# A small load on 120 partitions moved from the front of the load queue to second place, and its square from ScalarE to VectorE

The chip is one Trainium2, of which one core is used. The metric is the time of one execution in device microseconds.

## The reference

The input `x` is fp32, 32 x 256 x 4096. Of every four neighbouring values the root of the mean square is taken (p = 2), so the output is 32 x 256 x 1024:

```python
for i in range(out_length):
    window = np.abs(x[:, :, 4*i:4*i + 4]) ** p
    result[:, :, i] = (np.mean(window, axis=-1)) ** (1.0 / p)
```

134.22 MB are read and 33.55 MB are written. There is very little arithmetic for each byte.

## The kernel before

The input is treated as one flat row of values. Nearly all of it is loaded in 22 large loads, most of them 128 partitions x 13184 values (6.75 MB), into three slots. ScalarE squares a load in three chunks, VectorE sums groups of four, ScalarE takes the root, and the results of two loads are stored at once. The 22 loads leave 840 x 128 values over, the "piece". It is 430 KB, 0.3% of the input. It lies on 120 partitions of 896 values and has its own load, sums and store.

```python
def load(i):
    ...
    nc.sync.dma_start(out=v, in_=block(xf, g, 1)[:, src:src + w])
...
def root(g, o, ends):
    nc.scalar.activation(out=o, in_=o, func=Act.Sqrt, scale=1.0 / k)
    if ends and g not in late:
        store(g, nc.scalar)
...
Q = 120
odd = ODD * P // Q
t = o_tiles[1][0:Q, 0:odd]
nc.sync.dma_start(out=t, in_=xf[(total - ODD) * P:total * P].rearrange("(p w) -> p w", p=Q))
ahead = 0
while ahead < n and loads[ahead][0] < X_SLOTS:
    load(ahead)
    ahead += 1
nc.scalar.activation(out=t, in_=t, func=Act.Square)
o = o_tiles[1][0:Q, odd:odd + odd // k]
nc.vector.tensor_reduce(
    out=o, in_=t.rearrange("p (n j) -> p n j", j=k),
    axis=mybir.AxisListType.X, op=mybir.AluOpType.add,
)
nc.scalar.activation(out=o, in_=o, func=Act.Sqrt, scale=1.0 / k)
nc.scalar.dma_start(
    out=of[(total - ODD) * P // k:total * P // k].rearrange("(p w) -> p w", p=Q), in_=o,
)
...
for i in range(n):
    ...
    for step in chunks:
        v = xs[i][:, c:c + step]
        nc.scalar.activation(out=v, in_=v, func=Act.Square)
        total_sum(ots[g][:, summed:summed + step // k], v, i)
        while pending and pending[0][0] <= done - LAG:
            root(*pending.pop(0)[1:])
        ...
```

## Time and profile before

| | before |
|---|---|
| time, median of 3 runs | 394.59 us (394.59 to 394.62) |
| span of the profiled run | 392.8 us |
| VectorE busy | 271.8 us (69%) |
| ScalarE busy | 292.5 us (74%) |
| bytes moved, mean rate | 167.79 MB, 427 GB/s |

### The profile page before, as it was taken

What the parts mean: (1) busy time and instruction counts of PE and PEld (TensorE: products, weight loads), DVE (VectorE), ACT (ScalarE), POOL (GpSimd) and SP (SyncE); (2) the same over time, 40 slices, a digit from 0 to 9 for tenths busy, and PEclk for the clock granted to TensorE, in tenths of its full rate; (3) what the DMA queues carried; (4) which work ended last, traced back from release to release, by engine and by line L of the source; (5) the groups of instructions that cost most, each with busy time, mean ns of one, the idle gap of its engine ahead of it and who ended that gap; (6) DMA issues with size and microseconds to landing.
All of it is one profiled execution on the core that took longest, in us unless ns stands there. A gap on an engine that the chain in (4) does not pass through costs nothing.

```text
span 392.8 us, 341 instructions
## 1 busy us (share of the span) xinstructions
DVE 271.8 (69%) x77; ACT 292.5 (74%) x128; POOL 0.2 (0%) x4
## 2 busy tenths in 40 slices
DVE  1059989594959495949594959495949494778781
ACT  3088987776776777677867786868586859899990
POOL 0000000000000000000000000000000000000000
DMA  9999999999999989999999999999999999999997
GB/s 361 420 429 446 446 446 384 430 470 430 389 432 473 430 387 435 467 430 422 432 435 430 427 435 427 430 435 459 459 404 430 459 438 430 395 430 432 429 432 315
DMA packets 5024, 167.79 MB, mean 427 GB/s; under 512 B 558, under 2 KB 678, under 8 KB 926
## 3 DMA queue, kind: packets, MB, share of 16 engines
q1 hardware_dynamic: 3879, 144.04, 85.2%
q10 hardware_dynamic: 1143, 23.73, 14.0%
q14 instruction: 2, 0.02, 0.0%
HBM read 134.22 MB, written 33.55 MB: 427 GB/s over the span
## 4 chain that ended last, share of the span: by engine, by line
DMA 62%; ACT 21%; DVE 10%; issue 4%; SPq 0%; ACTq 0%
DMA xt<-in_x_dram 62%; ACT xt L143 17%; DVE ot L96 8%; ACT ot L89 3%; ACT xt L89 1%; DVE xt L105 1%; DVE xt L106 0%; ACTq L86 0%; SPq L80 0%; SPq L112 0%; ACTq L89 0%
## 5 line engine op out<-in xcount | busy, mean ns | idle before, releaser
L143 ACT ACTIVATE xt<-xt 128x4384 f32<-128x4384 f32 (+4 forms) x62 | 229.6, 3705 | 85.1 <-DMA xt<-in_x_dram 81.9
L96 DVE TENSOR_REDUCE ot<-xt 128x1096 f32<-128x4384 f32 (+1 forms) x48 | 227.0, 4731 | 90.1 <-ACT xt L143 89.8
L89 ACT ACTIVATE ot<-ot 128x1096 f32<-128x1096 f32 (+1 forms) x54 | 59.8, 1107 | 1.8 <-DVE ot L96 1.1
L105 DVE TENSOR_TENSOR xt<-xt 128x1648 f32<-128x1648 f32 (+4 forms) x14 | 28.4, 2032 | 16.0 <-ACT xt L143 16.0
L89 ACT ACTIVATE xt<-xt 128x824 f32<-128x824 f32 (+2 forms) x8 | 6.5, 817 | 1.9 <-DVE xt L106 1.9
L106 DVE TENSOR_TENSOR ot<-xt 128x1096 f32<-128x1096 f32 (+1 forms) x6 | 7.8, 1303 | 0.2
L106 DVE TENSOR_TENSOR xt<-xt 128x824 f32<-128x824 f32 (+2 forms) x8 | 7.5, 939 | 0.3
L119 DVE TENSOR_REDUCE ot<-ot 120x224 f32<-120x896 f32 x1 | 1.1, 1086 | 5.7 <-ACT ot L117 5.7
L117 ACT ACTIVATE ot<-ot 120x896 f32<-120x896 f32 x1 | 0.9, 949 | 2.7 <-DMA ot<-in_x_dram 2.7
L117 ACT ACT_TABLE_LOAD x1 | 1.3, 1283 | 0.7 <-PEq L174 0.7
L123 ACT ACT_TABLE_LOAD x1 | 1.3, 1283 | 0.0
L123 ACT ACTIVATE ot<-ot 120x224 f32<-120x224 f32 x1 | 0.4, 389 | 0.0
L174 POOL MEMSET const-bfloat16-1.0<- 128x1 bf16 x1 | 0.1, 101 | 0.0
L174 POOL MEMSET const-uint8-127<- 128x1 uint8 x1 | 0.1, 101 | 0.0
L174 POOL MEMSET const-float32-0.0<- 128x1 f32 x1 | 0.1, 99 | 0.2 <-issue 0.2
L174 POOL MEMSET const-float32-1.0<- 128x1 f32 x1 | 0.1, 99 | 0.0
## 6 DMA issues: line engine op xcount, KB each, us to landing
xt<-in_x_dram SPq DMA_DIRECT2D x18, 6592.0 KB, 39.9
out_dram<-ot ACTq DMA_DIRECT2D x7, 3296.0 KB, 27.6
xt<-in_x_dram SPq DMA_DIRECT2D x3, 3296.0 KB, 29.4
out_dram<-ot SPq DMA_DIRECT2D x2, 3296.0 KB, 30.0
out_dram<-xt SPq DMA_DIRECT2D x1, 2472.0 KB, 10.4
xt<-in_x_dram SPq DMA_DIRECT2D x1, 2108.0 KB, 26.8
out_dram<-xt SPq DMA_DIRECT2D x1, 527.0 KB, 7.1
ot<-in_x_dram SPq DMA_DIRECT2D x1, 420.0 KB, 4.0
```

The source lines that it names most:

```text
L89: nc.scalar.activation(out=o, in_=o, func=Act.Sqrt, scale=1.0 / k)
L96: nc.vector.tensor_reduce(out=o, in_=v.rearrange("p (n j) -> p n j", j=k), axis=mybir.AxisListType.X, op=add,)
L105: nc.vector.tensor_tensor(out=h, in0=q[:, :, 0:2], in1=q[:, :, 2:4], op=add)
L106: nc.vector.tensor_tensor(out=o, in0=h[:, :, 0], in1=h[:, :, 1], op=add)
L117: nc.scalar.activation(out=t, in_=t, func=Act.Square)
L119: nc.vector.tensor_reduce(out=o, in_=t.rearrange("p (n j) -> p n j", j=k), axis=mybir.AxisListType.X, op=mybir.AluOpType.add,)
L123: nc.scalar.activation(out=o, in_=o, func=Act.Sqrt, scale=1.0 / k)
L143: nc.scalar.activation(out=v, in_=v, func=Act.Square)
L174: nc = _bacc.Bacc("TRN2", target_bir_lowering=False, num_devices=1)
```

## The change

The piece is loaded second, behind the first large load, so that the large load starts sooner. Its square goes to VectorE, and its compute is placed behind the first Square of the first large load. The bytes, the sums and the store stay.

```diff
-    t = o_tiles[1][0:Q, 0:odd]
-    nc.sync.dma_start(out=t, in_=xf[(total - ODD) * P:total * P].rearrange("(p w) -> p w", p=Q))
-    ahead = 0
+    odd_x = o_tiles[1][0:Q, 0:odd]
+    odd_o = o_tiles[1][0:Q, odd:odd + odd // k]
+    load(0)
+    nc.sync.dma_start(
+        out=odd_x, in_=xf[(total - ODD) * P:total * P].rearrange("(p w) -> p w", p=Q),
+    )
+    ahead = 1
...
-    nc.scalar.activation(out=t, in_=t, func=Act.Square)
...
+    def odd_sum():
+        nc.vector.tensor_tensor(out=odd_x, in0=odd_x, in1=odd_x, op=mybir.AluOpType.mult)
+        nc.vector.tensor_reduce(
...
+    def odd_root():
+        nc.scalar.activation(out=odd_o, in_=odd_o, func=Act.Sqrt, scale=1.0 / k)
+        nc.scalar.dma_start(
...
             nc.scalar.activation(out=v, in_=v, func=Act.Square)
+            if i == 0 and c == 0:
+                odd_sum()
             total_sum(ots[g][:, summed:summed + step // k], v, i)
             while pending and pending[0][0] <= done - LAG:
                 root(*pending.pop(0)[1:])
+            if i == 0 and c == 0:
+                odd_root()
```

More of the change, by code (lines that the diff above doesn't have):

```diff
@@ L116 @@
         ahead += 1
-    nc.scalar.activation(out=t, in_=t, func=Act.Square)
-    o = o_tiles[1][0:Q, odd:odd + odd // k]
-    nc.vector.tensor_reduce(
-        out=o, in_=t.rearrange("p (n j) -> p n j", j=k),
-        axis=mybir.AxisListType.X, op=mybir.AluOpType.add,
-    )
-    nc.scalar.activation(out=o, in_=o, func=Act.Sqrt, scale=1.0 / k)
-    nc.scalar.dma_start(
-        out=of[(total - ODD) * P // k:total * P // k].rearrange("(p w) -> p w", p=Q), in_=o,
-    )
+    def odd_sum():
+        nc.vector.tensor_tensor(out=odd_x, in0=odd_x, in1=odd_x, op=mybir.AluOpType.mult)
+        nc.vector.tensor_reduce(
+            out=odd_o, in_=odd_x.rearrange("p (n j) -> p n j", j=k),
+            axis=mybir.AxisListType.X, op=mybir.AluOpType.add,
+        )
+    def odd_root():
+        nc.scalar.activation(out=odd_o, in_=odd_o, func=Act.Sqrt, scale=1.0 / k)
+        nc.scalar.dma_start(
+            out=of[(total - ODD) * P // k:total * P // k].rearrange("(p w) -> p w", p=Q),
+            in_=odd_o,
+        )
     pending = []
```

## The prediction

> **What bounds the kernel now.** I first read the page's row of DMA share and the line on HBM traffic, then a table of stretches (busy time of each engine, DMA share, GB/s), then the chain of work that ended last, then the waits.
>
> ```profile
> DMA  9999999999999989999999999999999999999997
> HBM read 134.22 MB, written 33.55 MB: 427 GB/s over the span
> 20.00:340.00 320.00, 236.03 (x53) 246.34 (x101) 0.00 (x0) 1.00 1.00 431
> 340.00:380.00 40.00, 31.55 (x21) 38.96 (x20) 0.00 (x0) 1.00 1.01 432
> ```
>
> In the last two lines the columns are the stretch, its length, busy us of VectorE, ScalarE and GpSimd, the clock, the DMA share and GB/s. The transfers are full from 20 to 380 us, while VectorE is busy 74% (236/320) and ScalarE 77% (246/320). All 167.77 MB of input and output have to pass; at 431 GB/s that alone is 389 us of the 392.8 us span. What is left is the start (until data flows) and the end (the last results). The chain agrees: 62% of it is loads in flight. Its one long stretch of compute is the end: from 340.62 to 384.79 ScalarE runs almost without a gap, on loads that have landed, while late stores keep the transfers busy. That stretch starts when the load of 340.6 lands, so a delay or gain in the stream of loads should pass to the end, and one that only shifts compute in an early stage should not.
>
> The change touches only the first 45 us, so I looked at the timeline there.
>
> ```profile
> 0.72 1.28 ACT L117 ACT_TABLE_LOAD   x1 [0.72 <-PEq L174]
> 0.73 0.46 SPq L112 DMA_DIRECT2D ot<-in_x_dram  x1
> 1.24 1.30 SPq L80 DMA_DIRECT2D xt<-in_x_dram  x3
> 4.74 0.95 ACT L117 ACTIVATE ot<-ot 120x896 f32<-120x896 f32 x1 [2.73 <-DMA ot<-in_x_dram]
> 5.71 1.28 ACT L123 ACT_TABLE_LOAD   x1
> 5.72 1.09 DVE L119 TENSOR_REDUCE ot<-ot 120x224 f32<-120x896 f32 x1 [5.72 <-ACT ot L117]
> 7.00 0.39 ACT L123 ACTIVATE ot<-ot 120x224 f32<-120x224 f32 x1
> 7.42 0.64 ACTq L124 DMA_DIRECT2D out_dram<-ot  x1
> 20.36 7.63 ACT L143 ACTIVATE xt<-xt 128x4416 f32<-128x4416 f32 x2 [12.97 <-DMA xt<-in_x_dram]
> ...
> 36.00 3.88 ACT L143 ACTIVATE xt<-xt 128x4416 f32<-128x4416 f32 x1 [1.06 <-DMA xt<-in_x_dram]
> ```
>
> All compute on the small piece is done by 8 us, in a gap in which both engines wait for the first large load, which lands at 20.36. It costs the end nothing. Only its transfer, in front of everything, can cost anything.
>
> [...]one engine has no part of the piece. The trace agrees: by 10 us it counts 15 packets under 512 B (the completions of the small load) and 120 data packets under 8 KB, 8 for each of 15 engines.
>
> ```profile
> DMA packets 199, 3.81 MB, mean 381 GB/s; under 512 B 15, under 2 KB 15, under 8 KB 135
> ```
>
> [...]the load at 5.71 ends at 6.99 and the Sqrt starts at 7.00.
>
> **The change part by part.**
>
> Compute. One 949 ns Square leaves ScalarE, one multiply of 120x896 comes to VectorE[...]. From the trace's own two sizes (824: 1016 ns, 1648: 1875 ns, so 1.0425 ns an element) it is 1016 + 72 x 1.0425 = 1091 too. The 1086 ns reduction, the 389 ns Sqrt, the store and probably the second table load move from before 8 us to behind the first Square of the first large load. There ScalarE is needed: 1.28 (table) + 0.39 (Sqrt) + 0.64 (issue of the store) = 2.31 us are put in front of the second Square. I follow that stage with the trace's durations. Say the first large load lands at 18.8 (20.36 less some 1.5, next part). Square 18.8 to 22.7; the inserted work to 25.0; second Square to 28.8; Sqrt of the first chunk (its sum was done at 27.4) to 29.9; third Square to 33.7; Sqrt to 34.8. The second large load lands at about 35.7 to 36.0, so ScalarE still waits for it about 1 us. Before, it had waited 1.07 us for VectorE between second Square and first Sqrt; that wait is filled. VectorE ends the third sum at 33.7 + 4.7 = 38.4, against 38.69 before, so the slot of that load is free, and the fourth load issued, at the same time as before. Even if it were later: the third load lands at 51.55, so some 12 us of transfers are still queued then. The small piece lands at about 20 to 20.5, its multiply and sum end at 22.7, when VectorE gets its first large chunk. Cost of all this on the path: 0.
>
> Transfer. This is the part with an effect. Two stretches at the start:
>
> ```profile
> 1.70:2.00 0.30, 0.00 (x0) 0.30 (x1) 0.00 (x0) 1.00 1.20 215
> 2.00:2.90 0.90, 0.00 (x0) 0.01 (x1) 0.00 (x0) 1.00 0.81 271
> DMA packets 86, 0.31 MB, mean 257 GB/s; under 512 B 0, under 2 KB 0, under 8 KB 86
> DMA packets 65, 0.97 MB, mean 878 GB/s; under 512 B 15, under 2 KB 15, under 8 KB 49
> ```
>
> The third line is the DMA view of 1.7 to 2.9, the fourth that of 2.9 to 4.0. Bytes are counted where a packet starts. Until 2.9 only small data packets have started (86 of 120, each 3584 B); the other 34 and the first 16 packets of the large load (65 - 49 = 16, one for each engine, 52.7 KB each) start in 2.9 to 4.0, so on the mean at about 3.45. The rate before 2.9 is 257 GB/s, 60% of 431. Also the engine without a part of the small piece sits idle until 2.9 at least.
>
> After: the large load is issued at 0.73, and its first packets should start when those of the small piece do now, at 1.7 to 2.0, mean 1.85: 1.6 us sooner. The first packets of a stream are slower: 1.20 x 0.30 x 16 / 18 packets = 0.32 us each in 1.7 to 2.0, against 0.81 x 0.90 x 16 / 68 = 0.17 us after. That start-up of 0.15 us stays, now on large packets. Then the small piece has to pass in mid stream: 8 packets x 0.17 = 1.37 us on 15 engines, at best 28.7 KB at 431/16 GB/s = 1.06 us. Say 1.2. Sum: 1.6 - 0.15 - 1.2 = 0.25 us gained in the stream, 0.1 to 0.4 by the choice of the packet's time. The slowest engine decides a landing, and the start would have a spread of 0.3 us (1.7 to 2.0) in place of 1.1 (2.9 to 4.0), which may give some 0.2 more. I take 0.3 us. The large loads then land 0.3 sooner all the way to 340.6, and the end with them: 394.59 - 0.3 = 394.3.
>
> **The rivals.** (1) Stall on ScalarE and VectorE: [...]if the small piece lands late (its small packets queue behind long ones), the first sum and the second Square wait for it. For: it now lies behind 6.75 MB. Against: it follows in the same queue and needs about 1.2 us more. Even 3 us of it would be absorbed by the 12 us of queued loads and by ScalarE's 23% of free time: 394.3 to 394.7. (2) A large load needs longer from issue to first packet than a small one: for it speaks that no large packet started before 2.9 even on the idle engine, 1.66 us after its issue at 1.24, against 1.0 us for the small piece[...]. Then the start is at 2.4, not 1.85, and the sum is 0.25 - 0.55, a loss of 0.3: 394.9. (3) The small load hides wholly, because its packets overlap with the large ones around it: gain 1.6 - 0.15 = 1.45: 393.1. Against: [...]the bytes still have to pass. (4) The store of the piece, issued at 25 in place of 7.4, collides with the first large store of 56.5: it took 20.7 us to land before, so it should be gone by 46. No effect.
>
> **Range and chances.** Main case 394.3; rival 2 in part gives up to 394.8; the slowest-engine argument or part of rival 3 down to 393.8. The three runs before lie within 0.03 us, so noise adds little. All cases lie far inside 2% (7.9 us): faster 0.01, same 0.98, slower 0.01.
>
> **What would show it.** Right: first large packets at about 1.8; first large load landing near 18.8 in place of 20.36; second load at 35.7; VectorE x78 and ScalarE x127 instructions; the multiply 1.09 us; a table load of 1.28 us behind the first large Square; ScalarE idle before the second load's Square; load of 340.6 some 0.3 us sooner, and the span by the same. Wrong: a first landing later than 19.5 (rival 2); second load at 36.0 or later, which says the order of the queue is worth nothing; ScalarE without a gap before the second load; or a shift at 340.6 that differs from the one at 36, which would mean that the middle isn't a rigid stream of transfers.

1.6 - 0.15 - 1.2 = 0.25 us gained, taken as 0.3 with a part of the estimate for the slowest engine, so 394.59 - 0.3 = 394.3 us. What is cut is:

- the rule from which 15 engines were worked out. The trace shows the 15: it counts 15 completions of the piece, and 16 of each large load.
- That nothing can be won in the middle was not shown. Shown is a DMA share of 1.00 at 431 GB/s from 20 to 340 us.
- The 1091 ns stand on the two sizes in the trace, and the changed kernel's page has 1092 ns.
- The load at 5.71 that ends at 6.99 is ScalarE's table load (1283 ns).

That the slowest engine decides a landing shows in the kernel before: the last of the first large load's 16 semaphore increments comes at 20.34, and the Square starts at 20.36.

## The result

The changed kernel takes 395.51 us (median of 6 runs, 395.28 to 395.65) against 394.61 us for the kernel before in the same rounds (6 runs, 394.59 to 394.63). The ratio is 1.0022, with a 95% interval of 1.001 to 1.0035. The change is clearly within 2%, and it is a small loss of 0.9 us where a gain of 0.3 us was predicted.

The page after, in lines that answer to those of before (the DMA row in 40 slices, the HBM traffic):

```profile
span 393.8 us, 342 instructions
DMA  8999999999999999999999999999999999999997
HBM read 134.22 MB, written 33.55 MB: 426 GB/s over the span
```

The bytes are the same and the rate is 1 GB/s lower. The timeline of the start shows where:

```profile
0.73 0.38 SPq L80 DMA_DIRECT2D xt<-in_x_dram  x1
1.17 0.47 SPq L114 DMA_DIRECT2D ot<-in_x_dram  x1
...
20.53 3.88 ACT L152 ACTIVATE xt<-xt 128x4416 f32<-128x4416 f32 x1 [18.52 <-DMA xt<-in_x_dram]
22.34 1.09 DVE L123 TENSOR_TENSOR ot<-ot 120x896 f32<-120x896 f32 x1 [22.34 <-DMA ot<-in_x_dram]
...
24.43 1.28 ACT L130 ACT_TABLE_LOAD   x1
24.47 4.74 DVE L96 TENSOR_REDUCE ot<-xt 128x1104 f32<-128x4416 f32 x1
25.72 0.39 ACT L130 ACTIVATE ot<-ot 120x224 f32<-120x224 f32 x1
26.14 0.64 ACTq L131 DMA_DIRECT2D out_dram<-ot  x1
26.82 3.86 ACT L152 ACTIVATE xt<-xt 128x4384 f32<-128x4384 f32 x1 [0.71 <-ACT ot L130]
...
37.88 3.88 ACT L152 ACTIVATE xt<-xt 128x4416 f32<-128x4416 f32 x1 [1.30 <-DMA xt<-in_x_dram]
```

The first large load is issued at 0.73 in place of 1.24, yet ScalarE can start on it only at 20.53, against 20.36 before. One engine makes it so late: of the 16 increments of that load's semaphore, 15 come at 18.30 to 19.63 (the mean of all is 18.95, against 20.06 before), and the last comes at 20.50 (before: 20.34). On the second load ScalarE starts at 37.88, against 36.00: already 1.88 us late. The compute went as predicted (the table load, Sqrt and store in front of the second Square), and ScalarE still waits 1.30 us for the second load, so compute isn't what is late. At the last load that ScalarE waits for, the shift is 0.97 us (the timelines of before, then of after):

```profile
340.62 3.88 ACT L143 ACTIVATE xt<-xt 128x4416 f32<-128x4416 f32 x1 [1.19 <-DMA xt<-in_x_dram]
```

```profile
341.59 3.88 ACT L152 ACTIVATE xt<-xt 128x4416 f32<-128x4416 f32 x1 [1.19 <-DMA xt<-in_x_dram]
```

So 1.9 us are lost by 38 us, and nearly 1 us of that comes back later.

**Packets.** The trace records start, duration and size of each DMA packet. It doesn't name the engine; I followed packets from the end of one to the start of the next. In the steady middle a large packet of 52736 B takes 1.947 us, which is 27.09 GB/s for one DMA engine. I counted for each stretch how much longer its packets took than their bytes at that rate, and divided by 16 engines. I call this the loss of a stretch:

```
us lost per engine      0-6    6-17   17-24  24-48  56-64
before                  0.95   0.03   0.04   0.03   0.43
changed                 0.81   0.05   1.27   0.09   0.02
```

(48 to 56 us lose 0.02 at most in both.) The 17 to 24 us stretch is where the piece passes. Its 120 packets took 0.205 us each (0.132 us would be their bytes at 27.09 GB/s), and the first large packet behind them on each engine took 2.62 us on the mean, in place of 1.95. The second thing is at 56 to 64 us, where the first large store begins: the kernel before loses 0.43 us there, the changed one almost nothing. This is a part of what comes back.

The engines also drift apart. The 16 completions of the second load lay within 0.72 us before and within 2.09 us in the changed kernel. A load has landed when its slowest engine has (the last increment of the second load's semaphore in the changed kernel comes at 37.86, and ScalarE starts at 37.88), so on the mean the engines are 0.99 us late there (36.25 in place of 35.26), but the landing is 1.88 us late.

### The profile page after: what moved, and what is told of

It is laid out like the page before. It is cut to its first block, busy times and chain, and to the rows that moved or that the text cites. A ratio compares the mean times of both kernels' runs of the same rounds, so it can differ in the third digit from the quotient of the medians. Undisturbed runs are those within 1.5% of the kernel's fastest.

```text
span 393.8 us, 342 instructions
## 1 busy us (share of the span) xinstructions
DVE 272.9 (69%) x78; ACT 291.6 (74%) x127; POOL 0.2 (0%) x4
## 4 chain that ended last, share of the span: by engine, by line
DMA 59%; ACT 24%; DVE 11%; issue 4%; another core or an unknown queue 0%; ACTq 0%; SPq 0%
DMA xt<-in_x_dram 59%; ACT xt L152 19%; DVE ot L96 10%; ACT ot L89 4%; ACT xt L89 1%; DVE xt L105 1%; DVE xt L106 0%; ACTq L86 0%; SPq L114 0%; SPq L80 0%; ACTq L89 0%
## 5 line engine op out<-in xcount | busy, mean ns | idle before, releaser
L123 DVE TENSOR_TENSOR ot<-ot 120x896 f32<-120x896 f32 x1 | 1.1, 1092 | 22.3 <-DMA ot<-in_x_dram 22.3
L152 ACT ACT_TABLE_LOAD x1 | 1.3, 1283 | 0.7 <-PEq L187 0.7
L130 ACT ACT_TABLE_LOAD x1 | 1.3, 1283 | 0.0
## 6 DMA issues: line engine op xcount, KB each, us to landing
xt<-in_x_dram SPq DMA_DIRECT2D x1, 2108.0 KB, 26.8
```

The lines of the kernel that those rows point to most:

```text
L123: nc.vector.tensor_tensor(out=odd_x, in0=odd_x, in1=odd_x, op=mybir.AluOpType.mult)
L130: nc.scalar.activation(out=odd_o, in_=odd_o, func=Act.Sqrt, scale=1.0 / k)
```

## The experiments

The first theory (A) was that the block of small packets costs more in mid stream than at the front, since a cold start is paid anyway at the front (the slow first packets: 0.95 us lost from 0 to 6 us in the kernel before). The rivals were the moved compute (B), the plain bytes (C), the engine without a part of the piece (D), and later the layout of the piece (H). Each kernel was run five times (one six times), beside the kernel before.

### The two halves of the change

The order changed, the square still on ScalarE:

```diff
-        nc.vector.tensor_tensor(out=odd_x, in0=odd_x, in1=odd_x, op=mybir.AluOpType.mult)
+        nc.scalar.activation(out=odd_x, in_=odd_x, func=Act.Square)
```

> The changed kernel with one thing put back: the piece of 120 partitions is squared on ScalarE (949 ns) and not on VectorE; its load stays second. Theory A (the whole loss comes from where the small load stands in the queue): as the changed kernel, 395.3 to 395.7 us. Rival B (the loss comes from the moved compute, the stall of ScalarE and VectorE behind the late small piece): the multiply on VectorE is part of it, so the time moves by some tenths.

Measured: 395.50 us (before 394.71 in these rounds; ratio 1.0017, interval 1.0005 to 1.003). The loss of 17 to 24 us is 1.32.

The compute changed, the piece loaded first:

```diff
-    load(0)
     nc.sync.dma_start(out=odd_x, ...)
-    ahead = 1
+    ahead = 0
```

> The changed kernel with the load of the small piece put back to the front; the multiply on VectorE and the compute behind the first large chunk stay as changed, with the table load, Sqrt and store that delay the second large Square. Theory A (order of the loads): as the kernel before, 394.5 to 394.8 us, engines apart by 0.6 to 1.2 us in their completions. Rival B (moved compute): as the changed kernel, 395.3 to 395.7.

Measured: 394.60 us (ratio 0.9995, interval 0.9983 to 1.0008), loss of 17 to 24 us 0.02, completions of the second load within 0.74 us. The two runs agree: the order of the loads makes the whole loss, and the moved compute costs nothing. Rival B falls.

### What the piece costs in second place

```diff
-    nc.sync.dma_start(out=odd_x, ...)
+    nc.vector.memset(odd_x, 1.0)
```

> The changed kernel without the load of the small piece (a memset in its place, so that part of the result is wrong on purpose). Theory A: the piece in second place costs more than its bytes: eight small packets on an engine of some 0.2 us (1.45 us) and a first large packet behind them that takes 2.6 us in place of 1.95 us; without it the time is 395.5 - 2.1 = 393.4 us, and the second large load lands near 35.8 in place of 37.9. Rival C (the piece costs its bytes, 1.06 us, and the rest of the loss is the slow cold start on large packets): 394.4 us.

Measured: 393.80 us (ratio 0.9975, interval 0.9962 to 0.9987; the part of the result that the piece makes is wrong on purpose, and the check of the result let it pass). That lies between the two. The second load shows more than the total does: its completions are at 33.93 us on the mean, 2.32 us before those of the changed kernel. So the piece costs 2.3 us there, its bytes 1.0 (1.06 us on 15 of 16 engines), as theory A has it. But at the first store this kernel loses 1.03 us, where the changed one loses 0.02, and so only 1.7 us of the total remain.

### The same packets, alternating with large ones

```diff
-    nc.sync.dma_start(out=odd_x, ...)
+    nc.scalar.dma_start(out=odd_x, ...)
```

> The changed kernel with the small load issued on the ScalarE queue, so that its packets alternate with large ones of the other queue and don't come as a block. Theory A: no block of small packets, so no second slow large packet, and the piece costs about its bytes (1.06 us) or less; 395.5 - 1.0 = 394.5 us, perhaps 394.0. Rival C (a small packet costs its 0.2 us wherever it stands, and a large one behind it is slow): eight slow large packets on each engine, 396 us or more.

Measured: 396.26 us (ratio 1.0037, interval 1.0023 to 1.0051). This was a miss. The block is gone, the packets alternate one by one, the small ones take 0.15 us, and yet the large ones take 2.22 us on the mean from 6 to 17 us. It isn't the block, then, and it isn't the cold start. The small packets of this piece slow the large packets around them as a block in second place (2.62 us for the first large one behind) and one by one (2.22 us), against 1.95. Theory A was right in the amount but had no cause.

### The layout of the piece

The same bytes, still second, on 128 partitions:

```diff
-    Q = 120
+    Q = 128
```

> The changed kernel with the small piece laid out on 128 partitions of 840 (all 16 DMA engines, eight packets of 3360 B each) and still second. Theory A (small packets in the middle of large ones cost 0.2 us each and one slow large packet behind them, on every engine): as the changed kernel, 395.3 to 395.7 us. Rival D (the engine without a part runs ahead, the others are uneven, and that is what costs): engines stay within about 1.2 us of each other and the time comes near the one before, 394.6.

Measured: the loss of 17 to 24 us is 0.08 in place of 1.27. The small packets take 0.132 us (their 3360 B would be 0.124 at 27.09 GB/s), and the large ones behind them 1.95. The second load is complete at 34.98 us on the mean, 0.28 us sooner than in the kernel before: this is the gain that was predicted, to 0.03 us. Theory A in its first form (any small packets cost) is refuted. The stretch of 16 to 26 us in the table of stretches (length, then busy us of VectorE, ScalarE, GpSimd, the clock, the DMA share, GB/s), for the kernels before and changed:

```profile
16.00:26.00 10.00, 1.72 (x1) 5.64 (x2) 0.00 (x0) 1.00 1.00 429
```

```profile
16.00:26.00 10.00, 3.62 (x3) 5.45 (x3) 0.00 (x0) 1.00 1.01 381
```

and for the changed kernel on 128 partitions:

```profile
16.00:26.00 10.00, 4.66 (x3) 6.03 (x4) 0.00 (x0) 1.00 1.05 449
```

The DMA engines are as busy in the second (share 1.01) as in the others, but move less: their packets last longer. The DMA view of 17.7 to 21.5 us says it in packets, for the changed kernel on 120 and on 128 partitions:

```profile
DMA packets 167, 1.27 MB, mean 335 GB/s; under 512 B 31, under 2 KB 31, under 8 KB 151
```

```profile
DMA packets 190, 2.01 MB, mean 530 GB/s; under 512 B 32, under 2 KB 32, under 8 KB 160
```

(A packet's bytes are counted where it starts, so a short window can show more than the real rate.) Both windows hold the whole piece: 151 - 31 = 120 small packets, and 160 - 32 = 128. In the same time the second starts 0.74 MB more of the next load.

The total was 395.19 us (394.63 to 395.31; ratio 1.0008, interval 0.9996 to 1.0021), because this kernel loses 1.05 us at the first store. I come back to that.

128 partitions differ from 120 in two things: all 16 engines have a part (D; the window above counts 16 completions of the piece, beside 16 of the first large load, and the one on 120 partitions 15 beside 16), and the piece lies on the same 128 partitions as the large loads (H, the layout). The next two are to tell them apart. First, 112 partitions, 112 packets, which the author took to be seven for each of 16 engines; no count for this run is at hand that shows it:

```diff
-    Q = 120
+    Q = 112
```

> The changed kernel with the piece on 112 partitions of 960[...]. Theory H[...]: the stretch from 17 to 24 us loses about 1 us as with 120 partitions, large packets behind the piece of 2.3 us on the mean, and the time is 395.2 to 395.7. Rival D (one engine left out): no loss there, large packets of 1.95 us, as with 128 partitions.

Measured: loss of 17 to 24 us 1.15, small packets of 0.219 us (3840 B, 0.142 at 27.09 GB/s), the first large one behind them on each engine 2.53 us; 395.32 us (ratio 1.0016, interval 1.0004 to 1.0029). Rival D falls, if all 16 engines had a part. The table of stretches:

```profile
16.00:26.00 10.00, 4.33 (x3) 5.65 (x4) 0.00 (x0) 1.00 1.03 396
```

Second, 32 partitions, with few and larger packets:

```diff
-    Q = 120
+    Q = 32
```

> The changed kernel with the small piece on 32 partitions of 3360: the same bytes, still second, in two packets of 13.4 KB on each engine. Multiply and sum on VectorE grow to some 3.5 us each. Theory A, in the form that the small size of the packets costs: the phase takes 1.0 us in place of 1.45 and the large packet behind it is hardly slowed (0.1 in place of 0.65): 395.5 - 1.0 = 394.5 us. Rival E (any interruption of the large packets makes the next one slow, whatever its size): 395.5 - 0.45 = 395.0 or more.

Measured: 395.92 us (ratio 1.0026, interval 1.0013 to 1.004), loss of 17 to 24 us 1.83: worse than with small packets, and worse than either expectation. The 13440 B packets take 0.50 us as long as few engines are at them, which is 26.8 GB/s, and 1.00 us on the median of all 32, which is half of that.

Why the number of partitions matters was not shown. The trace has no record of where an engine writes. Another number of partitions also changes which part of `x` each engine reads, and the size of the packets, and no run tells these apart. What is shown is that 112, 120 and 32 partitions lose 1.15 to 1.83 us, and 128 loses 0.08.

The alternating queue again, on 128 partitions:

```diff
-    Q = 120
+    Q = 128
```

> The run with the piece on the ScalarE queue, but on 128 partitions. Theory H: the alternating small packets take 0.13 us and the large ones between them stay at 1.95 us (2.2 us with 120 partitions); the first large load is done on all engines by some 19.5 us in place of 22.3, and the time is below 395.2 us. Rival C (any small packet between two large ones slows the next): 396 us as before.

Measured: 395.08 us (ratio 1.0013, interval 0.9999 to 1.0026). The large packets of 6 to 17 us take 1.954 us in place of 2.221, and the first load is complete on all engines by 19.95 us. This is as theory H has it. The stretch of 10 to 16 us with 120 and with 128 partitions on the ScalarE queue:

```profile
10.00:16.00 6.00, 0.00 (x0) 0.00 (x0) 0.00 (x0) 1.00 0.86 327
```

```profile
10.00:16.00 6.00, 0.00 (x0) 0.00 (x0) 0.00 (x0) 1.00 1.05 449
```

### The place of the piece

```diff
-    load(0)
+    load(0)
+    load(1)
     nc.sync.dma_start(out=odd_x, ...)
-    ahead = 1
+    ahead = 2
```

> The changed kernel with the small load third, behind the second large load, and its compute behind the first chunk of that second load (the piece lies at the end of its buffer so that nothing waits for it). Theory A (the block costs the same wherever it stands in the stream): 395.3 to 395.7 us, the loss of 1.2 us now between 33 and 40 us. Rival F (it costs because it is second[...]): 394.4 us or less, as bytes alone would have it.

Measured: 395.24 us (ratio 1.0013, interval 1.0001 to 1.0026); the loss of 17 to 24 us is 0.01 and that of 24 to 48 us 1.11. The loss moves with the piece. (The compute of the piece moved with it, and its place in the buffer.)

At the front, with 32 and then with 128 partitions (each is the kernel before with another value of Q):

> The kernel before (piece first) with the piece on 32 partitions: two packets of 13.4 KB on each engine in place of eight of 3.6 KB on 15. Theory A (small packets cost): the start loses 0.95 us to the steady rate now; with larger packets some 0.3 us less, and the time is 394.3 us. Rival G (the cold start costs some 0.8 us whatever comes first): 394.5 to 394.6, no change.

Measured: 394.63 us (ratio 1.0002, interval 0.999 to 1.0015), loss of 0 to 6 us 1.05 against 0.95. The expectation of a gain was wrong: fewer and larger packets gained nothing here, in another layout that, like the one on 120 partitions, isn't that of the large loads.

> The kernel before (piece first) with the piece on 128 partitions. Theory H[...]: small packets of 0.13 us at the start in place of 0.19, and a first large packet that is less slowed; the first large load is done 0.3 to 0.5 us sooner on the mean, and the time is 394.1 to 394.3 us. Rival (the cold start costs the same whatever comes first): 394.6.

Measured: 394.82 us (ratio 1.0008, interval 0.9995 to 1.002). The start did get better, the loss of 0 to 6 us is 0.60 and the first large packet takes 2.02 us in place of 2.33, and the second load is complete 0.35 us sooner (34.91 on the mean). The total isn't better: the first store costs 0.80 us here.

### The first large store

Every version that comes to 58 us without a loss in mid stream pays 0.4 to 1.05 us between 56 and 64 us, and every version that lost 1.1 us or more in mid stream pays 0.02 or less. The large packets slow down there shortly before the first packets of the store start (in the kernel before, those that start from 58 to 60 us take 2.07 us in place of 1.95; the first store packet starts at 60.58). The kernels that didn't pay had issued that store at 57.8 us or later. How far apart the engines are doesn't decide it alone: at the third load the completions of the run on 112 partitions lay within 1.13 us and it lost 0.02, those of the run on 128, second, within 1.33 us and it lost 1.05. Two tries were made at the moment of the store. All stores one chunk later, piece second on 128 partitions (the core of the diff):

```diff
+        if held:
+            store(held.pop(), nc.scalar)
         if ends and g not in late:
-            store(g, nc.scalar)
+            held.append(g)
```

> The changed kernel with the piece on 128 partitions, and each store of the ScalarE queue issued one chunk later (some 4.8 us). With 128 partitions the block in the middle lost nothing, but the stretch of 56 to 64 us, where the first large store comes in, lost 1.05 us to slow large packets (0.43 in the kernel before, 0.01 in the changed one). Theory I (that loss hangs on the moment at which the store comes): it goes or shrinks, and the time is 394.2 to 394.6. Rival J (it hangs on how far apart the engines are, 1.3 us here): the same loss some 5 us later, 395.2.

Measured: 395.01 us (ratio 1.0008, interval 0.9995 to 1.002). The loss is 0.50 in 56 to 64 us and 0.21 in 64 to 76: a little less, and later. Neither expectation fits cleanly. The store was issued at 60.6 us, so a late moment alone isn't enough to lose nothing.

Then the first store alone delayed, in three orders (the piece also lies at the end of its buffer in these runs):

```diff
+        if ends and g == 0:
+            for _ in range(2):
+                nc.scalar.activation(out=odd_x, in_=odd_x, func=Act.Square)
         if ends and g not in late:
             store(g, nc.scalar)
```

> The changed kernel with the piece on 128 partitions, at the end of its buffer, and two Squares on data that is no longer needed (0.9 us each) in front of the first large store, so that it is issued at about 58.5 us in place of 56.8. Theory I (the loss of 1.05 us at the first store hangs on its moment): the stretch of 56 to 64 us loses less than 0.1 us, and the time is 394.1 to 394.4 us. Theory J (it hangs on something else, such as how the engines stand to each other): 395.1 us.

> The kernel before with the piece on 128 partitions and the same delay of the first large store, from 56.1 to about 58 us. Theory I: the 0.8 us lost there go, and the time is 393.9 to 394.2 us. Theory J: 394.7 to 394.8.

> The kernel before with nothing but the same delay of the first large store (the piece stays first, on 120 partitions, at the end of its buffer), from 56.5 to about 58.3 us. Theory I: the 0.43 us lost there go, and the time is 394.2 us. Theory J: 394.6.

Measured: 395.35, 395.53 and 394.90 us (ratios 1.0017, 1.0019, 1.0008), with losses of 0.74, 0.75 and 0.60 us in 56 to 64 us. The store was issued at 57.5, 57.1 and 57.4 us, so the delay came out at 0.6 to 0.9 us in place of the 1.7 to 1.9 intended, and short of 57.8. These runs show that a small delay doesn't help; they don't rule out that the moment has a part. What decides this loss stays open.

No correct version beats the kernel before beyond its interval.

## Why the prediction was wrong

**What held.** The transfers bound the kernel. The compute part cost nothing, with the instruction counts (78 on VectorE, 127 on ScalarE), the multiply of 1.09 us, the place of the second table load and a waiting ScalarE before the second load all as predicted. The first large packets did start at 1.75 to 2.35 us; the mean is 1.93 where 1.85 was predicted. A loss in the stream did pass to the end, though not the whole of it. The chances were right: the change is within 2%.

**The step that failed** is the one that let the small piece "pass in mid stream" at "8 packets x 0.17", "say 1.2", with nothing lost by the large packets around it. With the other terms beside it, for the second load on the mean:

| term | predicted, us | measured, us |
|---|---|---|
| large packets start sooner | -1.6 | -1.54 (3.46 to 1.93) |
| start-up stays on large packets | +0.15 | +0.39 (first packet 2.72, before 2.33) |
| the piece in mid stream | +1.2 | +1.54 (8 x 0.205 us on 15 of 16 engines) |
| first large packet behind the piece | none | +0.67 (2.62 in place of 1.95) |
| sum | -0.25 | +1.06 (completions: +0.99) |

The sign was lost in the last two terms. Both come from the layout: on 128 partitions the piece takes 8 x 0.132 us, the large packets behind it take 1.95 us, and the completions come 0.28 us sooner than before. That this is so near the 0.25 of the prediction is luck in part, since the start-up was mis-sized as well. Nor does the layout settle the total: 128 partitions took 395.19 us, 0.5 more than the kernel before in the same rounds (within the interval), and lost 1.05 us at the first large store, for a reason that stays open. I had seen that the piece on 120 partitions has 15 engines (15 completions in the trace), and stopped there, without asking what the layout does to the packets around it.

**The rivals.** Rival 2 (a late first packet) didn't come about: the first large packets start 1.20 us after their issue on the mean, where it wanted 1.66. But they last 0.39 us longer than before, which is part of the loss. Rival 1 (a stall of compute) cost nothing, as was argued. Rival 3 (the small load hides) is refuted, since leaving the piece out moves the second load by 2.3 us. Rival 4 looked at the wrong store: that of the piece did no harm, while the first large store costs some kernels up to 1.05 us, and this moved nearly every total.

**The slack for the slowest engine** went the wrong way. The prediction gave 0.2 us for a smaller spread of engines; the spread of the second load grew from 0.72 to 2.09 us. In one mark the prediction named its own failure: "a first landing later than 19.5" and "second load at 36.0 or later" both came about. The first of them wasn't by rival 2, to which the prediction had tied it, but by the one slow engine: on the mean the first load had landed at 18.95, near the predicted 18.8. There was also a shift at 340.6 (0.97) that differs from that at 36 (1.88), which means that the middle is no rigid stream. The completions were 0.99 us late on the mean at the second load and 0.77 at the load of 340.6, so only 0.2 us net had come back for the engines together (0.41 at the first store, less what was lost again later). The rest is the slowest engine: it trails the mean by 1.12 and then 1.04 us in the changed kernel, but by 0.28 and then 0.82 in the kernel before, which had got a straggler too.

## What to carry to other kernels

Where transfers bound a kernel, look at the layout of a small load and not only at its bytes: in mid stream the same bytes lost 0.08 us on 128 partitions and 1.15 to 1.83 on 112, 120 or 32. The load on fewer partitions did best at the very front (394.6 us on 120 and on 32), where no large packets are in flight yet (in the kernel before, 86 of the 120 small packets start by 2.9 us, and the first large one at 2.95). No layout won time in total here: a term saved at one place was taken back at the next boundary of the stream, so read the loss stretch by stretch and not only from the total.
